# First stage of a two-block forward pass: input squares added on VectorE, block inverses of both directions joined, chunk matrices stored from GpSimd

## The chip, the core and the metric
One core of one Trainium2 chip runs the whole program in one launch. The metric is device time in microseconds, from start to end of the launch. Three runs of the kernel before took 2054.11, 2059.92 and 2060.92 us, so its median is 2059.92 us. Engines have short names in the rows: PE is TensorE (PEld its weight loads), DVE is VectorE, ACT is ScalarE, POOL is GpSimd, SP is SyncE, which here only issues DMAs.

## The reference, cut to what matters
Two transformer blocks over 1024 positions of width 1024, batch 1, in float32. The change lies in the first block, whose parts are

```python
h = rms_norm(x, norm_w)                       # sum of squares over the 1024 inputs
proj = h @ w_in                               # q, k, v, z, gates of the delta rule; q, k, v, z of attention
q, k = rotary(rms_norm(q)), rotary(rms_norm(k))   # windowed attention with sinks
m = where(strict, (k_beta @ k.T) * decay, 0)  # delta rule, chunk by chunk, forward and backward
t_inv = triangular_solve(eye + m, eye)        # unit triangular inverse of each chunk
u, w = t_inv @ (v * beta), t_inv @ (k_beta * exp(g))
a_intra = where(incl, (q @ k.T) * decay, 0)
```

where `decay` is exp of a difference of cumulated log gates. A scan over the chunks, an output norm, the output product and the second block follow; they are not touched.

## The kernel before, in words
The inputs are kept transposed: 8 row blocks of 128 input features (index k) by two halves of 512 positions (index h), 16 tiles of 128x512 in all. Each float32 operand of a projection is split into a rounded part and a rest (`hi`, `lo` for inputs, `wh`, `wl` for weights), and a product is the three matmuls of `mm3` (L219 to L221). The inputs are not scaled by the norm; its reciprocal `rcol` is applied when a product leaves PSUM.

The first stage runs in four parts, in the order of the code at the end of its block:

- `x_tile` loads the 16 tiles, splits them and sums their squares. Even k: ScalarE squares, VectorE adds (L746, L748). Odd k: GpSimd squares and adds (L744, L748). There are two sums for each half, and `norm_col` (L294) multiplies both with a column of ones; the result goes through `rsqrt` (L182 to L188), a chain of small VectorE steps, into `rcol`.
- Job `tg` (gates, attention keys and values), then `tq` twice (attention queries), each of 8 blocks of 128 positions. `kv_evac` and `q_evac` scale by `rcol`, square and sum by head (`sums`, L491, L492), and `rotated` (L496 to L512) applies norm weights and rotary tables, splits and transposes. `norm_row` spreads `rcol` to rows by copies `cb_a` (L302) and products `rb_a` (L303).
- Twelve jobs `fm` (delta rule q, k, v) with convolution and transposes, then `gate_terms`.
- Four jobs `ts`, `tz` (output gates). Between their matmuls stand the chunks: `m_chunk` makes for each of 8 chunks of 128 positions (two directions in one 128x512 tile, four heads) the decay `gam` from a product `pe`, the matrix `x_`, and two matrices `ta`; they are stored to `mdram` and `adram`. `base` reads the 16x16 diagonal blocks of four chunks back from `mdram` and inverts them by 15 rounds of a product `tmp` (L712) and a sum (L713), for each direction apart, starting from unit matrices that it loads (L706), and stores `cblk`.

The next stage needs the buffers of the first one, so its loads wait for the last `tz` matmul.

The order on each engine is not that of the code: a scheduler that runs a model of time while the program is built places the instructions. Every engine then works strictly in its own order, and an instruction that waits holds all behind it. DMAs issued from SP and ACT stand in those engines' orders too. Tags with a few buffers (`BUFS_A`) tie a writer to the last reader of the buffer.

Of the kernel before, what the change touches and what calls it, by code (L numbers as in the profile page):

```python
# [22 lines left out]
P = 128  # L23
# [10 lines left out]
BUFS_A = dict(wr=2, wh=6, wl=6, cv=4, acc=4, st=2, n1=4, n4=2, mb=1, tt=1, tmp=2)  # L34
# [78 lines left out]
def tile_two_blocks(ctx: ExitStack, tc: tile.TileContext, t, out, dbg=None, stop=None):  # L113
# [3 lines left out]
    dma, store = nc.sync.dma_start, nc.scalar.dma_start  # L117
# [308 lines left out]
    with ExitStack() as c1:  # L426
# [3 lines left out]
        def small(name, n, dt=F32):  # L430
# [15 lines left out]
        trir = pg.tile([P, 2, P], F32R, name="trir", tag="trir")  # L446
# [3 lines left out]
        GTr, LTr = trir[:, 0, :], trir[:, 1, :]  # L450
# [7 lines left out]
        with ExitStack() as ca:  # L458
# [15 lines left out]
            def tables():  # L474
                for nm, scale in (("k", 1.0), ("q", 0.125)):
                    wr = page("st", f"nw{nm}", [P, P])
                    dma(wr, t[f"swa_{nm}_norm_w"].partition_broadcast(P))
                    for i in range(2):
                        tb = page("cv", f"tab{nm}{i}", [P, NB, 64])
                        dma(tb, t["rope"][:, i])  # L480
                        if scale == 1.0:
                            G.tensor_tensor(tb, tb, rep(wr[:, i * 64 : (i + 1) * 64], NB), ALU.mult)
                        else:
                            if i == 0:
                                A.activation(wr, wr, AF.Copy, scale=scale)
                            G.tensor_tensor(tb, tb, rep(wr[:, i * 64 : (i + 1) * 64], NB), ALU.mult)
                        tabs[nm, i] = tb

            def sums(y, n, Hn, ss, name):
                sq = page("acc", f"sq{name}", [P, n, Hn, 64])  # L490
                G.tensor_tensor(sq, y, y, ALU.mult)  # L491
                V.tensor_reduce(ss, sq, AX.X, ALU.add)  # L492

            def rotated(y, rr, n, Hn, c, nm, name):
# [3 lines left out]
                for i in range(n):  # L498
                    G.tensor_tensor(t1[:, i], y[:, i], rep(tabs[nm, 0][:, c + i, :], Hn), ALU.mult)
                    for a in range(2):  # L500
                        V.tensor_tensor(
                            t2[:, i, :, 32 * a : 32 * a + 32], y[:, i, :, 32 - 32 * a : 64 - 32 * a],
                            rep(tabs[nm, 1][:, c + i, 32 * a : 32 * a + 32], Hn), ALU.mult,
                        )
                V.tensor_tensor(t1, t1, t2, ALU.add)
# [124 lines left out]
            def gate_terms():  # L630
# [13 lines left out]
                V.tensor_copy(ahi, av)  # L644
                V.tensor_tensor(alo, av, ahi.bitcast(F32), ALU.subtract)
# [15 lines left out]
            def m_chunk(gi, ci):  # L661
# [1333 lines left out]
```

## Time and profile before

| | us |
|---|---|
| median of three runs | 2059.92 |
| profiled execution | 2061.51 |
| its span, first to last instruction | 2059.5 |
| PE busy | 1943.0 (94%) |
| DVE busy | 1495.7 (73%) |
| ACT busy | 937.5 (46%) |
| POOL busy | 431.2 (21%) |

The profiled execution lies 1.6 us above the median, and its span 2.0 us below its own time. A share of busy time is a mean over stages with different limits, so the stage is to be read by stretches. The first stage is the first 398 us of the span.

### The profile page before, as it was taken

How to read it: one execution, taken by the hardware profiler on the slowest of the kernel's cores; microseconds unless marked ns; L12 is line 12 of the kernel's file. 1: busy time of each engine (PE TensorE's matmuls, PEld its weight loads, DVE VectorE, ACT ScalarE, POOL GpSimd, SP SyncE). 2: the span in 40 equal slices, each digit the busy share in tenths (PEclk: the TensorE clock that was granted, in tenths of full speed). 3: DMA queues.
4: the chain of work that ended last, by engine and by line, in shares of the span. 5: the costliest groups of instructions: out<-in, count | busy, mean ns of one | idle time of the engine just before them, and what ended most of it. 6: DMA issues, size and time to landing. Idle time of an engine off the chain costs nothing.

```text
span 2059.5 us, 31630 instructions
## 1 busy us (share of the span) xinstructions
PE 1943.0 (94%) x11446; PEld 1691.6 (82%) x11446; DVE 1495.7 (73%) x3087; ACT 937.5 (46%) x1954; POOL 431.2 (21%) x453
## 2 busy tenths in 40 slices
PE   6899988989988999799999799999999999999999
PEld 6888888889987789798999687686888888888887
DVE  7888888377797469563364888538977777776987
ACT  4446543134344253125553566525545445444443
POOL 5320073255252113011020762111000000000000
PEclk9999999999999999999999999999999999999999
DMA  5132334324535626743222223611222222267332
GB/s 167 41 122 75 89 113 129 98 52 144 150 105 191 233 82 181 238 140 101 61 85 59 79 65 89 226 49 59 84 92 82 72 92 82 72 214 277 98 97 83
DMA packets 177548, 235.13 MB, mean 114 GB/s; under 512 B 52944, under 2 KB 94064, under 8 KB 177392
## 3 DMA queue, kind: packets, MB, share of 16 engines
q1 hardware_dynamic: 148464, 205.84, 31.6%
q10 hardware_dynamic: 28928, 27.27, 4.0%
q8 instruction: 90, 1.47, 0.3%
q14 instruction: 66, 0.54, 0.1%
HBM read 174.86 MB, written 58.20 MB: 113 GB/s over the span
## 4 chain that ended last, share of the span: by engine, by line
PE 70%; DVE 15%; DMA 7%; issue 3%; ACT 3%; POOL 1%; SPq 0%; DVEq 0%; ACTq 0%; POOLq 0%
PE upx L219 4%; PE upx L220 4%; PE upx L221 4%; PE up L220 3%; PE up L221 3%; PE up L219 3%; DMA wa<-in_w_ada 2%; PE fm L220 2%; PE fm L219 2%; PE fm L221 2%; PE dnx L220 2%; PE dnx L219 2%; PE dnx L221 2%; PE apo L1241 1%; PE apt L1234 1%
## 5 line engine op out<-in xcount | busy, mean ns | idle before, releaser
L1587 ACT ACTIVATE uh<-wu 128x512 fp32r<-128x512 f32 x154 | 94.5, 628 | 143.0 <-DMA wu<-in_w_up 52.8
L1725 DVE SCALAR_TENSOR_TENSOR u<-c,fcw,u 128x1023 f32<-128x1023 f32 (+1 forms) x88 | 112.5, 1278 | 10.2 <-ACT u L1723 10.0
L1588 DVE TENSOR_TENSOR ul<-wu,uh 128x512 fp32r<-128x512 f32 x154 | 105.6, 698 | 4.7 <-ACT uh L1587 4.6
L210 DVE TENSOR_TENSOR wl<-wr,wh 128x512 fp32r<-128x512 f32 (+1 forms) x100 | 74.8, 755 | 43.9 <-ACT wh L209 43.3
L209 ACT ACTIVATE wh<-wr 128x512 fp32r<-128x512 f32 (+1 forms) x100 | 62.5, 630 | 94.6 <-PE fm L220 19.7
L403 DVE SCALAR_TENSOR_TENSOR aac<-wa,silc,aac 128x512 f32<-128x512 f32 x84 | 70.5, 839 | 37.1 <-DMA wa<-in_w_ada 32.6
L595 DVE SCALAR_TENSOR_TENSOR cacc<-raw,cw,cacc 128x512 f32<-128x512 f32 x96 | 70.5, 761 | 2.0 <-ACT cacc L593 0.6
L198 ACT ACTIVATE wdh<-w 128x512 fp32r<-128x512 f32 x55 | 34.8, 632 | 79.7 <-PE dnx L220 23.4
L220 PE MATMUL dnx<-bdl,wdh 128*128 128x512 f32 x176 | 68.6, 390 | 0.0
L221 PE MATMUL dnx<-bdh,wdl 128*128 128x512 f32 x176 | 68.5, 389 | 0.0
L1217 DVE CUSTOM_DVE_ANT_0 ass<-as,tb 128x512 f32<-128x512 f32 (+2 forms) x96 | 51.5, 552 | 23.4 <-PE as L1216 21.5
L1224 ACT ACTIVATE ass<-ass,amx 128x128 f32<-128x128 f32 (+3 forms) x64 | 49.3, 770 | 35.9 <-DVE amx L1223 33.8
L1723 ACT ACTIVATE u<-c,fcb,fcw 128x1024 f32<-128x1024 f32 x44 | 54.6, 1242 | 8.4 <-DVE c L1709 4.3
L199 DVE TENSOR_TENSOR bdl<-act,bdh 128x512 fp32r<-128x512 f32 x77 | 52.7, 684 | 1.8 <-ACT bdh L198 1.5
L220 PE MATMUL dny<-bdl,wdh 128*128 128x512 f32 x132 | 51.4, 389 | 0.0
L221 PE MATMUL dny<-bdh,wdl 128*128 128x512 f32 x132 | 51.4, 389 | 0.0
L836 ACT ACTIVATE ssb<-ssb,wnm 128x384 f32<-128x384 f32 (+1 forms) x64 | 36.8, 578 | 27.4 <-DVE wes L838 18.4
L219 PE MATMUL dnx<-bdh,wdh 128*128 128x512 f32 x176 | 48.9, 389 | 0.4 <-DVE dp L1898 0.4
L1234 PE MATMUL apt<-ident,ass 128*128 128x128 f32 x288 | 47.5, 280 | 1.7 <-ACT ass L1224 1.2
L198 ACT ACTIVATE bdh<-act 128x512 fp32r<-128x512 f32 x77 | 47.8, 621 | 2.1 <-issue 1.6
L863 PE MATMUL po<-sv,pTs 128*128 128x64 f32 x352 | 46.4, 271 | 1.5 <-DVE pTs L857 0.6
L199 DVE TENSOR_TENSOR wdl<-w,wdh 128x512 fp32r<-128x512 f32 x55 | 37.7, 686 | 13.4 <-ACT wdh L198 13.2
(2162 smaller groups left out, 7048.7 us busy)
## 6 DMA issues: line engine op xcount, KB each, us to landing
wu<-in_w_up SPq DMA_DIRECT2D x44, 512.0 KB, 3.3
wa<-in_w_ada SPq DMA_DIRECT2D x84, 256.0 KB, 3.5
adram<-u SPq DMA_DIRECT2D x22, 512.0 KB, 2.8
act<-adram SPq DMA_DIRECT2D x44, 256.0 KB, 5.6
wd<-in_w_down SPq DMA_DIRECT2D x20, 512.0 KB, 3.8
wr<-in_w_in_fm SPq DMA_DIRECT2D x24, 256.0 KB, 2.8
w<-in_w_down SPq DMA_DIRECT2D x22, 256.0 KB, 5.6
xt<-in_xT SPq DMA_DIRECT2D x16, 256.0 KB, 5.3
```

What stands on the lines that cost most here:

```text
L198: A.activation(hi, src, AF.Copy)
L199: marks["lo"] = V.tensor_tensor(lo, src, hi.bitcast(F32), ALU.subtract)
L210: V.tensor_tensor(lo, raw, hi.bitcast(F32), ALU.subtract)
L219: T.matmul(ps, ah, bh, start=first, stop=False, skip_group_check=more)
L220: T.matmul(ps, ah, bl, start=False, stop=False, skip_group_check=more)
L221: marks["mm3"] = T.matmul(ps, al, bh, start=False, stop=last, skip_group_check=more)
L403: V.scalar_tensor_tensor(aac, wa, silc[:, k : k + 1], aac, ALU.mult, ALU.add)
L595: V.scalar_tensor_tensor(acc, raw[h][:, j : j + H], cw[:, m, j : j + 1], acc, ALU.mult, ALU.add)
L1234: T.transpose(pt[:, u * P : (u + 1) * P], ss[i][:, g * P : (g + 1) * P], ident)
L1587: A.activation(hi, src, AF.Copy)
L1588: V.tensor_tensor(lo, src, hi.bitcast(F32), ALU.subtract)
L1725: V.scalar_tensor_tensor(u[:, sft:], cc[:, : S - sft], fcw[:, m, 2 - sft : 3 - sft], u[:, sft:], ALU.mult, ALU.add)
```

## The change
The squares are made by ScalarE for all k and added by VectorE into one sum for each half. The norm weight times rotary table is made by VectorE; the second table is loaded with its halves exchanged, in pieces of 32 numbers. `sums` squares on ScalarE. `rotated` makes both products over all blocks at once on VectorE and adds the halves crosswise. In `m_chunk` the gate is no longer split: `pe` is two float32 matmuls in place of four on rounded operands, one operand tile for each direction, both made by VectorE; `w1` is a ScalarE copy overwritten by a predicated VectorE copy under a byte mask; both `ta` are made by VectorE. The stores of `x_`, `ta` and `cblk` are issued from GpSimd. `base` holds the second direction reversed, so that one instruction serves both directions, and copies the unit matrices from a tile that is loaded once. GpSimd keeps some fills and casts and the diagonal fill and transposing copy at the end of `base`.

```diff
-    dma, store = nc.sync.dma_start, nc.scalar.dma_start
+    dma, store, pdma = nc.sync.dma_start, nc.scalar.dma_start, nc.gpsimd.dma_start
...
             def tables():
...
+                    tb = tabs[nm, 0] = page("cv", f"tab{nm}0", [P, NB, 64])
+                    dma(tb, t["rope"][:, 0])
+                    V.tensor_tensor(tb, tb, rep(wr[:, 0:64], NB), ALU.mult)
+                    tb = tabs[nm, 1] = page("cv", f"tab{nm}1", [P, NB, 64])
+                    for a in (0, 32):
+                        half = tb[:, :, a : a + 32]
+                        dma(half, t["rope"][:, 1, :, 32 - a : 64 - a])
+                        V.tensor_tensor(half, half, rep(wr[:, 96 - a : 128 - a], NB), ALU.mult)
...
-                G.tensor_tensor(sq, y, y, ALU.mult)
+                A.activation(sq, y, AF.Square)
...
-                for i in range(n):
-                    G.tensor_tensor(t1[:, i], y[:, i], rep(tabs[nm, 0][:, c + i, :], Hn), ALU.mult)
-                    for a in range(2):
-                        V.tensor_tensor(
...
-                V.tensor_tensor(t1, t1, t2, ALU.add)
+                tab = lambda i: tabs[nm, i][:, c : c + n, :].unsqueeze(2).to_broadcast([P, n, Hn, 64])
+                V.tensor_tensor(t1, y, tab(0), ALU.mult)
+                V.tensor_tensor(t2, y, tab(1), ALU.mult)
+                for a in (0, 32):
+                    half = t1[:, :, :, a : a + 32]
+                    V.tensor_tensor(half, half, t2[:, :, :, 32 - a : 64 - a], ALU.add)
...
-                    for part in (ahi.bitcast(F32), alo):
-                        r_ = page("n1", f"rr{c}{len(rr)}", G4, F32R)
-                        (G if d == 0 else V).tensor_tensor(r_, rep(mat, 4), bc(part[:, c, 4 * d : 4 * d + 4], P), ALU.mult)
-                        rr.append(r_)
-                w1, w2 = page("acc", f"w1{c}", G4), page("acc", f"w2{c}", G4)
-                G.tensor_tensor(w1, rep(LT, 4), bc(wgt[:, c, 0:4], P), ALU.mult)
-                G.tensor_tensor(w2, rep(GT, 4), bc(wgt[:, c, 4:8], P), ALU.mult)
-                V.tensor_tensor(w1, w1, w2, ALU.add)
+                    r_ = page("n1", f"rr{c}{d}", G4)
+                    V.tensor_tensor(r_, rep(mat, 4), bc(av[:, c, 4 * d : 4 * d + 4], P), ALU.mult)
+                    rr.append(r_)
+                w1 = page("acc", f"w1{c}", G4)
+                A.activation(w1, bc(wgt[:, c, 0:4], P), AF.Copy)
+                V.copy_predicated(w1, rep(gtm, 4), bc(wgt[:, c, 4:8], P))
...
-                for i, mat in enumerate((GTr, GTr, LTr, LTr)):
-                    T.matmul(pe, mat, rr[i], start=i == 0, stop=i == 3)
+                for i, mat in enumerate((GT, LT)):
+                    T.matmul(pe, mat, rr[i], start=i == 0, stop=i == 1)
...
-                dma(m_view(gi, ci), x_)
+                pdma(m_view(gi, ci), x_)
...
-                    (G if d == 0 else V).tensor_tensor(tt, gam, rep(mat, 4), ALU.mult)
-                    dma(adram[c, d], tt.rearrange("p h d -> p (h d)"))
+                    V.tensor_tensor(tt, gam, rep(mat, 4), ALU.mult)
+                    pdma(adram[c, d], tt.rearrange("p h d -> p (h d)"))
...
+                V.tensor_scalar(mb[:, 0].rearrange("p j i -> p (j i)"), raw, -1.0, None, ALU.mult)
+                V.tensor_scalar(mb[:, 1].rearrange("p j i -> p (j i)"), raw[:, ::-1], -1.0, None, ALU.mult)
                 tt = page("tt", f"tt{gi}", [P, 2, 16, 16])
-                for d in range(2):
-                    dma(tt[:, d].rearrange("p r c -> p (r c)"), t["eye16"].partition_broadcast(P))
+                A.activation(tt.rearrange("p d r c -> p d (r c)"), rep(eye, 2), AF.Copy)
                 for q in range(1, 16):
-                    for d in range(2):
...
+                    tmp = page("tmp", f"tmp{gi}{q}", [P, 2, 15, 15])[:, :, 0:q, 0:q]
+                    V.tensor_tensor(tmp, tt[:, :, 0:q, 0:q].rearrange("p d j c -> p d c j"), mb[:, :, 0:q, q].unsqueeze(2).to_broadcast([P, 2, q, q]), ALU.mult)
+                    V.tensor_reduce(tt[:, :, q, 0:q], tmp, AX.X, ALU.add)
...
                 for u in range(2):
-                    dma(cblk[gi, u].rearrange("(q r c) -> q r c", q=P, r=16), tt[:, u])
+                    pdma(cblk[gi, u].rearrange("(q r c) -> q r c", q=P, r=16), tt[:, u])
...
-                if odd:
-                    G.tensor_tensor(sq, xt, xt, ALU.mult)
+                if k == 0:
+                    xsum[h] = page("acc", f"xacc{h}")
+                    A.activation(xsum[h], xt, AF.Square)
                 else:
-                    A.activation(sq, xt, AF.Square)
-                if k >= 2:
-                    (G if odd else V).tensor_tensor(xacc[h][odd], xacc[h][odd], xt, ALU.add)
+                    A.activation(xt, xt, AF.Square)
+                    V.tensor_tensor(xsum[h], xsum[h], xt, ALU.add)
```

The code's edits also move instructions on the engines. The first place is VectorE's order around the norm chain of the first half of positions (`ru_n`, `rcol`), where `xacc` is the sum of squares, `x17l` the rest of the last tile and `tabq` the rotary table of the queries. Before:

```order
L210 TENSOR_TENSOR wl_288<-wr_286,wh_287 128x512
L188 SCALAR_TENSOR_TENSOR rcol<-ru_n_340,rcol 128x4
L748 TENSOR_TENSOR xacc_222<-xacc_222,xt_264 128x512
L186 TENSOR_TENSOR ru_n_340<-rcol 128x4
L737 SCALAR_TENSOR_TENSOR x17l<-xt_272,norm_w,x17h 128x512
L187 SCALAR_TENSOR_TENSOR ru_n_340<-ru_n_340,rv_n_338 128x4
L188 SCALAR_TENSOR_TENSOR rcol<-ru_n_340,rcol 128x4
L186 TENSOR_TENSOR ru_n_340<-rcol 128x4
L187 SCALAR_TENSOR_TENSOR ru_n_340<-ru_n_340,rv_n_338 128x4
L188 SCALAR_TENSOR_TENSOR rcol<-ru_n_340,rcol 128x4
L524 TENSOR_SCALAR gates<-tg_304,rcol 128x16
```

And VectorE's order there in the changed kernel:

```order
L739 TENSOR_TENSOR xacc_221<-xacc_221,xt_255 128x512
L188 SCALAR_TENSOR_TENSOR rcol<-ru_n_335,rcol 128x4
L739 TENSOR_TENSOR xacc_221<-xacc_221,xt_263 128x512
L186 TENSOR_TENSOR ru_n_335<-rcol 128x4
L480 TENSOR_TENSOR tabq_589<-tabq_589,nwq 128x512
L739 TENSOR_TENSOR xacc_221<-xacc_221,xt_271 128x512
L187 SCALAR_TENSOR_TENSOR ru_n_335<-ru_n_335,rv_n_333 128x4
L485 TENSOR_TENSOR tabq_592<-tabq_592,nwq 128x8x32
L188 SCALAR_TENSOR_TENSOR rcol<-ru_n_335,rcol 128x4
L186 TENSOR_TENSOR ru_n_335<-rcol 128x4
L485 TENSOR_TENSOR tabq_592<-tabq_592,nwq 128x8x32
L187 SCALAR_TENSOR_TENSOR ru_n_335<-ru_n_335,rv_n_333 128x4
```

More sums of squares and the products of the query table, which wait for the table's loads, now stand between the steps of the norm chain; the chain of the second half follows directly behind it.

The second place is VectorE's order where the copies `cb_a` for the row form of the norm stand among the query heads (`qy` scaled by its norm, `t1q`, `t2q` the rotary products). Before:

```order
L496 TENSOR_TENSOR qy_824<-qy_824,rrq_1023 128x512
L496 TENSOR_TENSOR qy_880<-qy_880,rrq_1023 128x512
L496 TENSOR_TENSOR qy_936<-qy_936,rrq_1023 128x512
L496 TENSOR_TENSOR qy_992<-qy_992,rrq_1023 128x512
L541 CAST khh_109<-ptk_725 64x128
L501 TENSOR_TENSOR t2q_1041<-qy_824,tabq_599 128x4x32 x4
L302 COPY cb_a_753<-rcol 128x128
L501 TENSOR_TENSOR t2q_1073<-qy_880,tabq_599 128x4x32
L541 CAST khh_108<-ptk_737 64x128
L501 TENSOR_TENSOR t2q_1073<-qy_880,tabq_599 128x4x32
L302 COPY cb_a_756<-rcol 128x128
```

And in the changed kernel:

```order
L302 COPY cb_a_733<-rcol 128x128
L187 SCALAR_TENSOR_TENSOR ru_dn<-ru_dn,rv_dn 128x32
L188 SCALAR_TENSOR_TENSOR rrq_1000<-ru_dn,rrq_1000 128x32
L494 TENSOR_TENSOR qy_801<-qy_801,rrq_1000 128x512
L494 TENSOR_TENSOR qy_857<-qy_857,rrq_1000 128x512
L494 TENSOR_TENSOR qy_913<-qy_913,rrq_1000 128x512
L494 TENSOR_TENSOR qy_969<-qy_969,rrq_1000 128x512
L497 TENSOR_TENSOR t1q_1017<-qy_801,tabq_589 128x512
L498 TENSOR_TENSOR t2q_1018<-qy_801,tabq_592 128x512
L497 TENSOR_TENSOR t1q_1046<-qy_857,tabq_589 128x512
L498 TENSOR_TENSOR t2q_1047<-qy_857,tabq_592 128x512
L302 COPY cb_a_738<-rcol 128x128
```

The third and fourth copies (`cb_a_730`, `cb_a_733`) now stand ahead of the four `qy`, and the next pair stands behind eight full instructions.

The third place is SP's order at the end of the chunks, where `mb` (now `mr`) is the read of the diagonal blocks. Before:

```order
L695 DMA adram<-ta_3327 128x512
L695 DMA adram<-ta_3324 128x512
L701 DMA mb_3330<-mdram 128x16x16
L720 DMA cblk<-tt_3081 128x256 x2
L706 DMA tt_3333<-in_eye 128x256 x2
L208 DMA wr_3927<-in_w_in_z 128x512
```

And in the changed kernel:

```order
L208 DMA wr_3491<-in_w_in_z 128x512
L208 DMA wr_3497<-in_w_in_z 128x512
L693 DMA mr_3174<-mdram 128x16x16
L208 DMA wr_3727<-in_w_in_z 128x512
```

No store and no load of unit matrices stands in SP's order any more.

## Rows read from the trace of the kernel before
**Rows 1.** The page: busy tenths in 40 slices of the span.
```profile
PE   6899988989988999799999799999999999999999
POOL 5320073255252113011020762111000000000000
```
**Rows 2.** Windows: busy us of each engine in five stretches, granted PE clock, DMA.
```profile
8.40:42.40 34.00, 25.55 (x163) 24.10 (x163) 33.51 (x45) 18.11 (x32) 23.78 (x17) 0.93 0.64 202
42.40:50.80 8.40, 8.40 (x48) 8.40 (x49) 2.01 (x3) 2.75 (x8) 3.38 (x3) 0.69 0.01 2
50.80:112.00 61.20, 54.39 (x438) 53.66 (x437) 47.01 (x138) 28.37 (x83) 21.64 (x28) 0.94 0.19 60
112.00:263.30 151.30, 151.30 (x731) 124.12 (x730) 132.09 (x270) 80.17 (x232) 13.91 (x33) 1.00 0.29 89
263.30:397.80 134.50, 119.61 (x925) 116.43 (x923) 94.27 (x200) 48.24 (x69) 59.44 (x44) 0.95 0.39 119
```
**Rows 3.** Timeline of PE: start us, us, instruction, idle before and what ended it.
```profile
60.19 0.39 PE L219 MATMUL tq<-wh,x00h 128*128 128x256 f32 x1 [1.14 <-ACT ky L529]
93.54 0.80 PE L303 MATMUL rb_a<-ident,cb_a 128*128 128x128 f32 x2 [5.10 <-DVE cb_a L302]
```
**Rows 4.** Timeline of DVE, 8 to 93 us.
```profile
28.85 1.78 DVE L737 SCALAR_TENSOR_TENSOR x15l<-xt,norm_w,x15h 128x512 fp32r<-128x512 f32 x1
33.69 1.25 DVE L183 TENSOR_SCALAR ri_n<-rv_n 128x4 int32<-128x4 int32 x1
36.21 1.18 DVE L186 TENSOR_TENSOR ru_n<-rcol 128x4 f32<-128x4 f32 x1
41.37 0.66 DVE L524 TENSOR_SCALAR gates<-tg,rcol 128x16 f32<-128x16 f32 x4
56.44 0.16 DVE L186 TENSOR_TENSOR ru_n<-rcol 128x4 f32<-128x4 f32 x1
87.94 3.55 DVE L496 TENSOR_TENSOR qy<-qy,rrq 128x512 f32<-128x512 f32 x4
```
**Rows 5.** Groups of DVE by shape, 0 to 62 us: busy us, mean ns.
```profile
L748 DVE TENSOR_TENSOR xacc<-xacc,xt 128x512 f32<-128x512 f32 x6 | 7.5, 1251 | 0.1
```
**Rows 6.** Groups of DVE by shape, 262 to 347 us.
```profile
L673 DVE TENSOR_TENSOR w<-w,w 128x512 f32<-128x512 f32 x8 | 10.3, 1290 | 1.9 <-POOL w L672 1.9
L668 DVE TENSOR_TENSOR rr<-tri,alo 128x512 fp32r<-128x512 f32 x7 | 10.1, 1436 | 0.0
L684 DVE TENSOR_TENSOR x<-pgr,gam 128x512 f32<-128x512 f32 x8 | 5.5, 682 | 0.7 <-ACT gam L679 0.7
```
**Rows 7.** Groups of POOL by shape, 260 to 350 us.
```profile
L671 POOL TENSOR_TENSOR w<-tri,wgt 128x512 f32<-128x512 f32 x8 | 12.0, 1495 | 5.8 <-DVE x L685 5.8
```
**Rows 8.** Waits of PE, 263 to 398 us: us in total, times, longest.
```profile
PE tz L220 <- DVE wl L210: 4.7, 1, 4.7
PE pe L677 <- DVE tmp L712: 4.1, 2, 2.5
PE ts L219 <- ACT s L573: 2.1, 1, 2.1
PE pqk L690 <- ACT gam L679: 2.0, 2, 1.1
```
**Rows 9.** Chain that ended last, 345 to 355 us: start us, us, what.
```profile
346.48 2.62 DMA cblk<-tt
349.57 4.43 DMA tt<-in_eye
```
**Rows 10.** Groups of PE by shape, 100 to 400 us; the third from the second block.
```profile
L677 PE MATMUL pe<-rr,trir 128*128 128x512 f32 x32 | 9.8, 418 | 6.0 <-DVE tmp L712 4.1 <-DVE x L684 1.9
L682 PE MATMUL pgr<-qk 128*128 128x128 f32 x64 | 8.7, 276 | 0.0
L1359 PE MATMUL pla<-glrT,wg 16*128 16x512 f32 x8 | 5.7, 851 | 4.2 <-DVE gl L1367 4.2
```
**Rows 11.** DMA issues, 300 to 400 us: KB each, median us to landing.
```profile
mdram<-x SPq DMA_DIRECT2D x5, 256.0 KB, 2.3
```

More of the change, by code (lines that the diff above doesn't have):

```diff
@@ L434, in tile_two_blocks @@
         ssk, ssq, rk, rkinv, rk2, rq = (small(n, 4) for n in ("ssk", "ssq", "rk", "rkinv", "rk2", "rq"))
-        beta, av, ahi, alo, wgt, neg, edec, egl, eg = (
-            small(n, 8, F32R if n == "ahi" else F32) for n in ("beta", "av", "ahi", "alo", "wgt", "neg", "edec", "egl", "eg")
-        )
+        beta, av, wgt, neg, edec, egl, eg = (small(n, 8) for n in ("beta", "av", "wgt", "neg", "edec", "egl", "eg"))
         rcol = pg.tile([P, NB], F32, name="rcol", tag="rcol")
@@ L449, in tile_two_blocks @@
         GT, LT, LE, GE = (tri[:, i, :] for i in range(4))
-        GTr, LTr = trir[:, 0, :], trir[:, 1, :]
         groups = ([0, 7, 1, 6], [2, 5, 3, 4])
@@ L477, in tables @@
                     dma(wr, t[f"swa_{nm}_norm_w"].partition_broadcast(P))
[L478 to L487, printed above, removed]
+                    if scale != 1.0:
+                        A.activation(wr, wr, AF.Copy, scale=scale)
+                    tb = tabs[nm, 0] = page("cv", f"tab{nm}0", [P, NB, 64])
[6 more added lines that the diff above has]
+                        V.tensor_tensor(half, half, rep(wr[:, 96 - a : 128 - a], NB), ALU.mult)
             def sums(y, n, Hn, ss, name):
                 sq = page("acc", f"sq{name}", [P, n, Hn, 64])
-                G.tensor_tensor(sq, y, y, ALU.mult)
+                A.activation(sq, y, AF.Square)
                 V.tensor_reduce(ss, sq, AX.X, ALU.add)
@@ L518, in kv_evac @@
                 if c == 0:
-                    norm_col(pbt, xacc[0], rcol[:, 0:4], "a0")
+                    norm_col(pbt, [xsum[0]], rcol[:, 0:4], "a0")
                     ys["ss"] = sm.tile([P, NB, 2], F32, name="ssk2", tag="ss2")
                 if c == 4:
-                    norm_col(pbt, xacc[1], rcol[:, 4:8], "a1")
+                    norm_col(pbt, [xsum[1]], rcol[:, 4:8], "a1")
                 r1 = rcol[:, c : c + 1]
@@ L716, in base @@
                 G.memset(tt[:, 1].rearrange("p r c -> p (r c)")[:, ::17], 0.0)
-                V.tensor_tensor(tt[:, 0], tt[:, 0], tt[:, 1], ALU.add)
+                V.tensor_tensor(
+                    tt[:, 0].rearrange("p r c -> p (r c)"), tt[:, 0].rearrange("p r c -> p (r c)"),
+                    tt[:, 1].rearrange("p r c -> p (r c)")[:, ::-1], ALU.add,
+                )
                 G.tensor_copy(tt[:, 1], tt[:, 0].rearrange("p r c -> p c r"))
                 for u in range(2):
-                    dma(cblk[gi, u].rearrange("(q r c) -> q r c", q=P, r=16), tt[:, u])
+                    pdma(cblk[gi, u].rearrange("(q r c) -> q r c", q=P, r=16), tt[:, u])
                 yield
@@ L728, in tile_two_blocks @@
             nw = load(pg, "norm_w", [P, NK], t["norm_w"])
-            xacc = [[None, None] for _ in range(2)]
+            xsum = {}
+            eye = page("eye", "eye", [P, 256])
             def x_tile(h, k):
@@ L738, in x_tile @@
                 xs[k][h] = (hi, lo)
-                odd = k % 2
-                if k < 2:
-                    xacc[h][odd] = page("acc", f"xacc{h}{k}")
-                sq = xacc[h][odd] if k < 2 else xt
-                if odd:
-                    G.tensor_tensor(sq, xt, xt, ALU.mult)
-                else:
-                    A.activation(sq, xt, AF.Square)
-                if k >= 2:
-                    (G if odd else V).tensor_tensor(xacc[h][odd], xacc[h][odd], xt, ALU.add)
+                if k == 0:
+                    xsum[h] = page("acc", f"xacc{h}")
+                    A.activation(xsum[h], xt, AF.Square)
+                else:
+                    A.activation(xt, xt, AF.Square)
+                    V.tensor_tensor(xsum[h], xsum[h], xt, ALU.add)
             def consts():
@@ L757, in consts @@
                 dma(tri, t["tri"])
+                dma(eye, t["eye16"].partition_broadcast(P))
                 dma(onw, t["dn_out_norm_w"].partition_broadcast(P))
-                G.tensor_copy(trir, tri[:, 0:2, :])
+                G.tensor_copy(gtm, GT)
                 for g in range(2):
```

20 lines of the change are left out of this document (5 added, 15 removed).

## The prediction
> **What bounds the kernel now.** I read the page's slices first [rows 1]: PE is near full almost everywhere, and POOL works above all in the first eight slices, which hold the first stage. Then the windows [rows 2], cut where the stage's parts begin and end. From 112 to 263.3 us PE is busy 151.30 of 151.30 us at full clock; nothing that the change touches can shorten this stretch, since its matmuls stay. PE's idle time lies elsewhere: 34.00 - 25.55 = 8.4 us up to 42.4, 61.20 - 54.39 = 6.8 us up to 112, and 134.50 - 119.61 = 14.9 us in the last stretch. To this comes the clock: after an idle stretch PE runs for a few us at the lower of its two levels (1.2 for 2.4 GHz); the granted share is 0.69 between 42.4 and 50.8, 0.94 and 0.95 in two longer ones. So the stage is bound by PE where PE is fed, and by VectorE where it is not: in the first window VectorE is busy 33.51 of 34.00 us.
>
> Why VectorE is slow there is seen in its own rows. A norm step of 128x4 numbers takes 1.25 and 1.18 us next to GpSimd's work, and 0.16 us at 56.44, where POOL stands still [rows 4]. Six additions of 128x512 have a mean of 1.25 us [rows 5]. In the chunks `w<-w,w` takes 1.29 and `rr` 1.44 us, while `x<-pgr,gam`, of the same size with one operand in PSUM, takes 0.68 us in the mean of eight and is never held up [rows 6]. GpSimd's instruction beside them takes 1.5 us [rows 7]. I take 0.68 us as the undisturbed length of a 128x512 instruction; such instructions overlap by some 0.08 us, so 0.6 us each in a row.
>
> **The change part by part.** All against the profiled execution's 2061.5 us.
>
> *Start, to the gates at 41.37 us [rows 4].* What goes: the six additions lose 6 x (1.25 - 0.68) = 3.4 us [rows 5]; four norm steps of the kind shown lose 1 us each, 4 us; five splits of inputs and two of weights of the kind of `x15l` (1.78 us [rows 4]) lose some 0.9 us each, 6 us. Sum 13.4 us. What comes: eight more additions, 8 x 0.6 = 4.8 us, and four table products' worth of 512 numbers, 2.4 us. Net -6 us on VectorE. The table products wait for loads, and the norm chain is queued behind them in VectorE's order; behind the chain stand the gates and the evacuations that give PE its PSUM back. The loads need buffers that the additions free late, so the last one lands some 3 us after its addition, against 1 to 2 us of work between them: I take back 1.5 us (bounds 0, and the whole 6 us if every table load is waited for). ScalarE gets eight more squares and a copy; at 18.11 us of 34 [rows 2] it takes 5 us more without being the bound. Net 4.5 us.
>
> *Second half's norm.* Its chain now follows directly, so PE's wait of 1.14 us at 60.19 [rows 3] goes: 1 us.
>
> *Row form of the norm.* PE waits 5.10 us for `cb_a` at 93.54 [rows 3], behind four `qy` that take 3.55 us [rows 4] and a run of `t2q`. In the new order a pair of copies stands ahead of them and the next pair eight instructions later (4.8 us), while PE has a block's 24 products between the pairs, 3 us. A wait of 1.5 us stays, 3.5 us go, and with them part of the stretch at the lower level that follows, which I put at 1 us: 4.5 us.
>
> *Fifteen rounds of `base`, other `rotated`, single norm sum.* `base` does the same numbers in half as many instructions, each now dependent on the one before; I put it at nothing, covered by other VectorE work between its steps; uncovered, 30 steps at 0.1 us would cost 3 us. `rotated` adds about 0.4 us for each call on VectorE, under PE's full stretch. Halving the norm's matmuls is worth under 1 us and lies in idle time: nothing.
>
> *Chunks.* On VectorE each chunk had 7 instructions and has 8 (one predicated copy for one addition, one `ta` more), 8 x 0.6 = 4.8 us more in all. The excess in [rows 6] goes: 8 x 0.6 + 7 x 0.75 = 10 us for two groups alone; with the other `rr`, `ta` and the small steps of `base` that I counted on the timeline it is 22 us. No row has a predicated copy; by the nearest rows it lies between 0.3 us, half of the undisturbed 0.68, and 1.4 us, the slowest two-operand group [rows 6], and I take 0.6. So VectorE gains 17 us here (11 to 20). PE pays: `pe` was four products, 9.8 / 8 = 1.2 us for a chunk. Float32 costs more: `pgr`, float32 with 512 columns in all, is 8.7 / 8 = 1.1 us, so two such are 2.2 us, +1.0 each and at most +8 in eight chunks; the other float32 row of 512 columns, partly at the lower level, is 5.7 / 4 = 1.4 us [rows 10], +13. I take 7 us, as part of these busy times is overlap.
>
> What PE can gain in this stretch is its 14.9 us of idle time and some 6 us for the clock (0.95 means that a tenth of 134.5 us ran at half speed). The `pe` waits, 4.1 us, should go; so should 4.7 us for `wl` [rows 8]. That one is VectorE held in its order by the load of unit matrices, 2.62 + 4.43 us after the blocks' store began [rows 9]; these loads no longer exist. What is late next is the read `mr` of the last chunks: it, the copy of the unit matrices and seven rounds stand ahead of the same `wl`, and by the old durations they fit into the 15 us that PE has work for, with about 2 us to spare. The waits for ScalarE's `s` and `gam`, 2.1 and 2.0 us, stay [rows 8]. Of 21 us I count 15 as regained, less 7 for `pe`: 8 us.
>
> *Stores from GpSimd.* 24 of `x_` and `ta`, 4 of `cblk`. SP's landing took 2.3 us [rows 11]. GpSimd has nothing else to do; no row shows a DMA issued there. Bounds: no more than SP's, so nothing, and 1.5 us each, the length of its arithmetic [rows 7], which makes 36 us spread over 60 us of chunks, still hidden. I take nothing, with the rival below.
>
> The Trainium skill weighs against this part: its page "SBUF — State Buffer" (section "SBUF: two separate sides") says that a DMA issued from GpSimd has its descriptors written there, and that these writes are locked out while VectorE runs certain copies in a two-port mode. The same page ("Who interferes with whom") counts `copy` and `tensor_scalar` among those, and not `tensor_tensor`. By it only the few sign changes of `base` would hold a store up, so the sum would be the same; the trace of before has no store from GpSimd and cannot say.
>
> Sum: 4.5 + 1 + 4.5 + 8 = 18 us, some 0.5 us more for stalls in between that I did not price: 2061.5 - 18.5 = 2043 for an execution like the profiled one, which lies 1.6 us above its median. So 2041 us. The order behind the first stage is nearly the old one, and I take no difference from it.
>
> **Rivals.**
> *The start gains nothing.* The table loads, in small pieces of 32 numbers, are waited for one after another, and the norm chain behind them is as late as before. For it: the order shown. Against it: the loads' queues are idle after 34 us. The chunks' 8 us and the row form's 4.5 us stay at best; with half of the latter, 2051 us.
> *The chunks gain nothing.* Float32 `pe` at the upper price, 13 us, eats what is regained, or VectorE with 64 us of work in a stretch of some 60 us of PE work stays the bound. For it: both engines come out almost equal. Then only the 10 us before remain: 2050 us.
> *Slower: stores from GpSimd become the bound.* If each takes over 2.5 us of GpSimd, 24 of them fill the 60 us of the chunks; `x_` and `ta` wait for their buffers, VectorE for them, PE for VectorE. Each further us costs 24 us. The rest of the gain, 18 us, is used up at about 3.3 us each; at 4 us it would be 2061 + 18 = 2077 us. For it: the page's rule, if it held for all of VectorE's work. Against it: SP's 2.3 us is mostly transfer, not issue.
> *It does not do what it says*: the diagonal fill and the transposing copy stay on GpSimd, but only twice; the rows show no other.
>
> **How the numbers follow.** My case has 0.62, 2041 us, own range 2032 to 2050. Start without gain 0.16, 2051. Chunks without gain 0.13, 2050. Slower 0.06, 2077. Nothing moves 0.03. More than my case is bounded by PE: all idle time but the first 8 us and all clock losses, less `pe`, would be some 29 us, 2031. The range 2030 to 2056 leaves out the slower rival and part of the tails. A change of over 0.3% (6.2 us), about what a measurement of this kernel can tell, means below 2053.7: 0.61 of my case, 0.11 and 0.11 of the two weaker ones, 0.83. Within 0.3%: 0.10. Slower: 0.07.
>
> **What would show it.** In the windows, the stretch up to the first `fm` matmul should be 10 us shorter, that of `ts`, `tz` and the chunks 8 us, the middle unchanged. No 128x4 step of VectorE above 0.3 us; `rr` and `ta` near 0.68 us. Gates near 37 us. The wait of `rb_a` under 2 us, none of `tz` for `wl`. `pe` above 1.9 us for a chunk. I am wrong if `tabq` is waited for by more than 3 us, if a store from GpSimd needs over 2.5 us before it starts, or if PE still idles over 8 us in the last stretch.

## The result and the profile after

The changed kernel takes 2026.14 us in the median of four runs, against 2059.53 us: ratio 0.984, interval 0.981 to 0.988. Two more comparisons gave 0.985 (0.982 to 0.987) and 0.984 (0.982 to 0.986). It is faster by 31 to 35 us, where 18.5 were forecast. Its profiled execution takes 2027.40 us (span 2025.6), 34.1 us less than that of before.

The page's slices of the changed kernel, against [rows 1]: POOL's first five slices are below a tenth, and PE's first seven at least as full as they were.

```profile
PE   7999999899989998899999899999999999999999
POOL 0000021563351123021022742110000000000000
```

The windows of the changed kernel, cut at the same events as [rows 2]; the columns are busy us of PE, PEld, DVE, ACT and POOL, PE's granted clock, the DMA share and GB/s:

```profile
8.40:37.90 29.50, 23.37 (x160) 22.03 (x160) 27.03 (x63) 22.23 (x41) 0.64 (x1) 0.96 0.74 225
37.90:50.80 12.90, 12.82 (x87) 12.82 (x88) 5.74 (x21) 8.95 (x24) 0.00 (x0) 0.82 0.15 43
50.80:102.80 52.00, 49.20 (x407) 49.01 (x406) 40.64 (x109) 29.05 (x81) 1.33 (x4) 0.97 0.21 71
102.80:253.20 150.40, 150.40 (x724) 123.50 (x724) 129.81 (x267) 81.43 (x231) 2.21 (x22) 1.00 0.29 88
253.20:373.70 120.50, 118.58 (x929) 111.02 (x928) 72.75 (x146) 50.99 (x75) 20.84 (x35) 1.00 0.46 137
373.70:474.90 101.20, 91.56 (x738) 87.78 (x737) 80.21 (x165) 36.30 (x93) 65.86 (x58) 0.95 0.27 76
```

The last three stretches of before, cut at the same events, for the comparison (the first of them ends with the first `ts` matmul, the second with the last `tz`, which starts at 399.66, 2 us behind the end of the last stretch of [rows 2]):

```profile
114.20:265.30 151.10, 151.10 (x727) 123.70 (x726) 131.85 (x269) 79.62 (x228) 15.57 (x35) 1.00 0.29 88
265.30:399.90 134.60, 119.71 (x927) 116.58 (x925) 92.33 (x198) 47.07 (x67) 57.78 (x43) 0.95 0.40 118
399.90:505.00 105.10, 93.91 (x739) 90.00 (x739) 81.43 (x167) 36.30 (x93) 66.39 (x58) 0.94 0.30 81
```

Read by these cuts, the time went so (all from PE's timelines of the two profiled executions, between starts of matmuls; `pc` is a product of the next stage):

| stretch | before | after | measured | forecast |
|---|---|---|---|---|
| start to first `fm` | 114.2 | 102.9 | -11.3 | -10 |
| first `fm` to first `ts` | 151.2 | 150.3 | -0.8 | 0 |
| first `ts` to last `tz` | 134.3 | 120.2 | -14.1 | -8 |
| last `tz` to last `pc` of the next stage | 104.3 | 100.4 | -3.9 | 0 |
| all behind it | 1555.6 | 1551.8 | -3.8 | 0 |

The last row is scatter: three traces of the changed kernel have 1551.8, 1558.2 and 1550.6 us there. In the first row 1.3 to 2.3 us of before are scatter too: three variants that leave the start as it was begin their first `fm` at 111.85 to 112.85. Between the means of the four traces with the old start and the ten with the new one lie 9.7 us. The third and fourth rows are larger than any scatter seen in them, and the forecast missed both.

VectorE's rows of the changed kernel at the start, against [rows 4]; no small step is above 0.2 us, and `gates` come at 36.97:

```profile
26.18 0.16 DVE L183 TENSOR_SCALAR ri_n<-rv_n 128x4 int32<-128x4 int32 x1
33.81 0.69 DVE L480 TENSOR_TENSOR tabq<-tabq,nwq 128x512 f32<-128x512 f32 x1 [0.73 <-DMA tabq<-in_rope]
36.97 0.66 DVE L520 TENSOR_SCALAR gates<-tg,rcol 128x16 f32<-128x16 f32 x4
```

VectorE's groups by shape, 0 to 62 us, against [rows 5], and 250 to 374 us, against [rows 6]:

```profile
L739 DVE TENSOR_TENSOR xacc<-xacc,xt 128x512 f32<-128x512 f32 x14 | 9.7, 691 | 0.1
...
L686 DVE TENSOR_TENSOR ta<-gam,tri 128x512 f32<-128x512 f32 x16 | 10.3, 684 | 0.1
L661 DVE TENSOR_TENSOR rr<-tri,av 128x512 f32<-128x512 f32 x12 | 8.1, 686 | 0.3 <-PE pe L669 0.3
L665 DVE COPY_PREDICATED w<-gtm,wgt 128x512 f32<-128x512 uint8 x8 | 5.9, 736 | 5.8 <-ACT w L664 5.8
L676 DVE TENSOR_TENSOR x<-pgr,gam 128x512 f32<-128x512 f32 x8 | 5.4, 677 | 0.0
```

PE's waits from 253 to 374 us, all that are left (us in total, times, longest), against [rows 8]:

```profile
PE pqk L682 <- ACT gam L671: 1.2, 2, 0.8
PE pf L600 <- ACT cacc L593: 0.4, 1, 0.4
PE pe L669 <- DVE x L676: 0.3, 1, 0.3
```

`pe` as a group of PE, 250 to 374 us, against [rows 10] (the trace has two records for each of the 16 float32 products):

```profile
L669 PE MATMUL pe<-rr,tri 128*128 128x512 f32 x32 | 15.3, 595 | 0.3 <-DVE x L676 0.3
```

The stores as groups of GpSimd in the same stretch (busy us, mean ns):

```profile
L687 POOL DMA_DIRECT2D adram<-ta x16 | 8.7, 542 | 8.9 <-DVE ta L686 8.3 <-issue 0.2
L678 POOL DMA_DIRECT2D mdram<-x x8 | 6.2, 780 | 59.4 <-DVE x L677 41.5 <-DVE tt L704 18.0
```

and as DMA issues (KB each, median us to landing), against [rows 11]:

```profile
adram<-ta POOLq DMA_DIRECT2D x16, 256.0 KB, 2.6
mdram<-x POOLq DMA_DIRECT2D x8, 256.0 KB, 2.8
cblk<-tt POOLq DMA_DIRECT2D x4, 128.0 KB, 3.4
```

### The profile page after: what moved, and what is told of

Same layout as the page of the kernel before. It is cut to its first block, busy times and chain, and to the rows that moved or that the text cites. A ratio compares the mean times of both kernels' runs of the same rounds, so it can differ in the third digit from the quotient of the medians.

```text
span 2025.6 us, 31441 instructions
## 1 busy us (share of the span) xinstructions
PE 1938.5 (96%) x11430; PEld 1683.3 (83%) x11430; DVE 1457.2 (72%) x3031; ACT 952.8 (47%) x1982; POOL 334.0 (16%) x389
## 4 chain that ended last, share of the span: by engine, by line
PE 74%; DVE 12%; DMA 7%; ACT 3%; issue 3%; SPq 1%; POOL 0%; ACTq 0%; DVEq 0%; POOLq 0%
PE upx L220 4%; PE upx L221 4%; PE upx L219 4%; PE up L220 3%; PE up L221 3%; PE up L219 3%; DMA wa<-in_w_ada 2%; PE fm L219 2%; PE fm L221 2%; PE fm L220 2%; PE dnx L220 2%; PE dnx L219 2%; PE dnx L221 2%; PE po L855 1%; PE apo L1233 1%
## 5 line engine op out<-in xcount | busy, mean ns | idle before, releaser
L828 ACT ACTIVATE ssb<-ssb,wnm 128x384 f32<-128x384 f32 (+1 forms) x64 | 36.8, 578 | 29.4 <-DVE wes L830 18.5
L855 PEld LDWEIGHTS po<-sv,pTs 128*128 128x128 f32 x352 | 46.3, 200 | 2.9 <-DVE pTs L849 1.4
```

The costliest lines, as they stand in the source:

```text
L855: T.matmul(po[:, h, :], pts[i][:, h, :], sv[:, kb, g * 64 : (g + 1) * 64], start=i == 0, stop=kb == kb1 - 1)
```

## The experiments

Those that begin with `b_` edit the kernel before, those with `a_` the changed one. In the three traces of the changed kernel the first 474 us repeat within 2 us, while the rest scatters over 8 us; so single parts are judged by PE's timeline in the first stage, and the time is given beside it.

**The changed kernel again.**

> The changed kernel once more, for its time against the kernel before and for a second trace. Theory: 2026 us (1.6% less than before), with 30 us of the difference ahead of the first matmul of the next stage's second part and nothing real behind it; the 3.8 us that the first pair of traces shows behind 505 us (of before) are then scatter between executions and come out between -4 and +4 here. Rival: the change moves the later stages too (other addresses of tiles, other order), and the same 3 to 4 us stand at the same places again.

> The changed kernel once more, beside its variant with the split gate on the same chip. 2024 to 2029 us; first fm matmul within 1 us of 102.6, first ts to last tz 120.2, both as in its two traces so far.

Measured: 2026.07 and 2025.15 us; first `fm` at 102.38 and 101.59, first `ts` to last `tz` 120.23 and 119.90, last `pc` at 473.2 and 472.0 (473.8 in the first trace). Behind it 1558.2 and 1550.6 us, against 1555.6 in the trace of before: 2.6 more and 5.0 less. The gain lies in the first 505 us; the later 3.8 us did not come again as such, as the theory said.

**One part at a time.** The start alone (the edits of `x_tile`, `tables`, `sums`, `rotated`):

```diff
-                G.tensor_tensor(sq, y, y, ALU.mult)
+                A.activation(sq, y, AF.Square)
...
+                V.tensor_tensor(t1, y, tab(0), ALU.mult)
+                V.tensor_tensor(t2, y, tab(1), ALU.mult)
```

> The kernel before with the part of the change ahead of the fm jobs alone: squares on ScalarE with one VectorE sum, tables multiplied on VectorE, sums and rotated as changed; chunks and base as before. Theory (the parts add up): first fm matmul at 103 us as in the changed kernel, 11 us earlier than before; the stretch from the first ts to the last tz matmul stays at 134 us and PE still waits 4 to 5 us for wl and 4 us at pe; in all 10 to 12 us less than before. Rival (a later wait takes the gain): the time falls by under 5 us, with the 11 us lost again in a longer stretch of ts and tz.

Measured: 2050.18 us against 2058.80, 8.6 less (ratio 0.996, 0.994 to 0.997), a little under the 10 to 12 expected. First `fm` at 104.17, 10.0 earlier than the profiled before and 7.7 to 8.7 earlier than in `b_addr`, `b_base` and `b_chunks`, which keep the old start; first `ts` to last `tz` 134.05. Nothing is taken back later. The two longest waits of PE, 250 to 392 us:

```profile
PE pe L676 <- DVE tmp L711: 6.4, 2, 3.3
PE tz L220 <- DVE wl L210: 5.0, 1, 5.0
```

The chunks' arithmetic alone, with stores on SP and `base` as before:

```diff
-                        (G if d == 0 else V).tensor_tensor(r_, rep(mat, 4), bc(part[:, c, 4 * d : 4 * d + 4], P), ALU.mult)
+                    V.tensor_tensor(r_, rep(mat, 4), bc(av[:, c, 4 * d : 4 * d + 4], P), ALU.mult)
...
-                    (G if d == 0 else V).tensor_tensor(tt, gam, rep(mat, 4), ALU.mult)
+                    V.tensor_tensor(tt, gam, rep(mat, 4), ALU.mult)
```

> The kernel before with the arithmetic of the chunks alone as changed: rr, the copy and predicated copy, both ta on VectorE, pe in two float32 products; stores stay on SP, base and the start as before. Theory (GpSimd's arithmetic beside VectorE held VectorE up): VectorE's 128x512 instructions take 0.68 us, the waits at pe (4.1 us) go, the wait of tz for wl (4.7 us) stays in some measure since base still loads its unit matrices: the stretch from first ts to last tz gets 6 to 9 us shorter than 134.3. Rival (the chunks gain only together with base): under 3 us shorter, since the small instructions of base keep VectorE as late as before.

Measured: 2048.14 us against 2058.80, 10.7 less (0.995, 0.993 to 0.996). The stretch from `ts` to `tz` is 126.00, 8.3 shorter. All of PE's waits in it:

```profile
PE tz L220 <- DVE wl L210: 5.6, 1, 5.6
PE pf L601 <- ACT cacc L594: 0.5, 1, 0.5
PE pqk L683 <- ACT gam L672: 0.3, 1, 0.3
```

The waits at `pe` are gone, and so are those for ScalarE's `s` and `gam` but for 0.3 us, which the forecast let stand; the wait behind the load of unit matrices stays.

`base` alone:

```diff
-                for d in range(2):
-                    dma(tt[:, d].rearrange("p r c -> p (r c)"), t["eye16"].partition_broadcast(P))
+                A.activation(tt.rearrange("p d r c -> p d (r c)"), rep(eye, 2), AF.Copy)
```

> The kernel before with base alone as changed: both directions in one instruction, unit matrices copied by ScalarE from a tile that is loaded once (into a part of rrow that is no longer read by then); chunks' arithmetic on GpSimd as before, stores on SP. The weights move by 2 KB too, so cmp is loaded early. Theory (the wait of 4.7 us for wl is the load of the unit matrices): this wait goes, the waits at pe stay within 1 us of 4.1, the stretch from first ts to last tz is 4 to 6 us shorter than 134.3. Rival (VectorE, held up by GpSimd, is the true cause of that wait): the stretch is under 2 us shorter.

Measured: 2048.66 us against 2058.80, 10.1 less (0.996, 0.994 to 0.997). The stretch is 129.68, 4.6 shorter. The wait of 4.7 us for `wl` is gone (1.1 us for `wh` is left). At `pe` PE waits 7.1 us:

```profile
PE pe L677 <- DVE x L684: 3.8, 3, 3.0
PE pe L677 <- DVE tmp L714: 3.3, 1, 3.3
```

That is no growth. The 4.1 us of my expectation are only the waits behind `tmp`; before has one more, behind `x`, which [rows 8] does not show (its 1.9 us stand in the first line of [rows 10]):

```profile
PE pe L677 <- DVE x L684: 1.9, 1, 1.9
```

So before waits 6.0 us at `pe`, and `b_addr` below, whose order is that of before, 7.1:

```profile
PE pe L677 <- DVE tmp L714: 6.5, 2, 3.4
PE pe L677 <- DVE x L684: 0.6, 2, 0.3
```

`base` also joins the two directions here, so the load of the unit matrices is not tested apart from that.

The parts add up: 8.3 + 4.6 = 12.9 of the 14.1 us of this stretch, and 10.0 of 11.3 at the start, both from the same late trace of before. The times of the three parts add up to 29.4 us of 31 to 35; in `b_base` half of the 10.1 us lies outside the stretch: its weights move too, and from the last `tz` to the last `pc` it takes 98.2 us against 104.3 before.

**Is it GpSimd's arithmetic as such, or waiting for its results?** First the stores back on SP, as a base for the two that follow:

```diff
-    dma, store, pdma = nc.sync.dma_start, nc.scalar.dma_start, nc.gpsimd.dma_start
+    dma, store, pdma = nc.sync.dma_start, nc.scalar.dma_start, nc.sync.dma_start
```

> The changed kernel with all stores of chunk matrices and block inverses issued from SP as before. Theory (the issuer is worth nothing, as predicted): within 2 us of the changed kernel; PE keeps under 3 us of idle time between the first ts and the last tz matmul. Rival (stores in SP's order hold up the loads of the weights and of mr, as the wait of 4.7 us for wl before): PE waits for wl again, 4 to 8 us more than the changed kernel.

Measured: 2029.40 us, beside 2026.07 of the changed kernel (ratios 0.987, 0.984 to 0.989, and 0.985, 0.982 to 0.987): 3.3 us more, where within 2 us was expected, and not told apart. First `ts` to last `tz` 119.93, last `pc` at 474.06, both as with GpSimd; PE waits 0.90 us for `wl`. The issuer is worth nothing in the first stage, though the stores land later from GpSimd: here from SP 2.2, 2.4 and 1.8 us after issue, from GpSimd 2.6, 2.8 and 3.4 (`ta`, `x_`, `cblk`).

Then products on GpSimd that nobody waits for:

```diff
+            nz = [rrow[:, 0:H], rrow[:, H:S]]
...
+                G.tensor_tensor(nz[0].rearrange("p (h d) -> p h d", h=4), rep(LT, 4), bc(wgt[:, c, 0:4], P), ALU.mult)
+                G.tensor_tensor(nz[1].rearrange("p (h d) -> p h d", h=4), rep(GT, 4), bc(wgt[:, c, 4:8], P), ALU.mult)
```

> The variant with stores from SP (a_sp), and in each chunk five products of 128x512 more on GpSimd, into a tile that nobody reads: as many as the kernel before had there. The order on the other engines is that of a_sp, and nothing waits for these products. Theory (GpSimd's arithmetic as such holds VectorE up): VectorE's instructions with both operands in SBUF (rr, x<-x,w, ta) rise from 0.69 to 1.1 to 1.4 us in the mean, those with one operand in PSUM stay at 0.68; PE waits again, the stretch from first ts to last tz matmul grows from 119.9 to 126 to 132 us and its clock falls under 1.00; time 6 to 12 us more. Rival (what cost time before was waiting for GpSimd's late results): the means stay, the stretch is less than 1 us longer.

Measured: 2046.07 us (ratio to before 0.993, 0.992 to 0.995), 17 to 21 us more than without. The window from first `ts` to last `tz`, of this variant:

```profile
254.40:391.70 137.30, 124.09 (x929) 113.56 (x928) 96.52 (x150) 52.75 (x79) 54.67 (x43) 0.96 0.41 124
```

and its groups of VectorE by shape, 250 to 380 us:

```profile
L692 DVE TENSOR_TENSOR ta<-gam,tri 128x512 f32<-128x512 f32 x16 | 15.4, 1004 | 0.1
L662 DVE TENSOR_TENSOR rr<-tri,av 128x512 f32<-128x512 f32 x12 | 14.9, 1264 | 0.0
L668 DVE COPY_PREDICATED w<-gtm,wgt 128x512 f32<-128x512 uint8 x8 | 10.9, 1359 | 1.4 <-ACT w L667 1.4
...
L681 DVE TENSOR_TENSOR x<-pgr,gam 128x512 f32<-128x512 f32 x8 | 5.4, 679 | 0.0
```

Nothing depends on these products, and VectorE's order is the same; yet its work in this stretch grows from 73 to 97 us, the clock falls to 0.96, and the stretch is 136.9 us long, more than expected and more than before the change (the mean of `ta`, 1.00 us, is a little under the range expected). The instruction with an operand in PSUM is untouched at 0.68 us. PE waits 8.4 us at `pe` for `x` and 1.5 for `gam` again; `a_sp` has neither wait. The rival is out.

Last, fills in place of the products:

```diff
-                G.tensor_tensor(nz[0].rearrange("p (h d) -> p h d", h=4), rep(LT, 4), bc(wgt[:, c, 0:4], P), ALU.mult)
+                G.memset(nz[0], 0.0)
+                G.memset(nz[0], 0.0)
```

> As a_noise, but with ten fills of 128x512 on GpSimd in each chunk in place of the five products: GpSimd writes as much and reads no operand. Theory (it is GpSimd's reading of operands that VectorE waits for): VectorE's means stay within 0.05 us of 0.69, the stretch from first ts to last tz stays within 1 us of 119.9. Rival (any access of GpSimd to SBUF will do): the means rise over 0.9 us and the stretch grows by 4 us or more.

Measured: 2029.19 us. The window of this variant:

```profile
253.90:373.90 120.00, 118.65 (x928) 111.01 (x928) 73.28 (x146) 50.89 (x75) 36.21 (x77) 1.00 0.47 138
```

and two of the same groups of VectorE:

```profile
L662 DVE TENSOR_TENSOR rr<-tri,av 128x512 f32<-128x512 f32 x12 | 8.2, 688 | 0.4 <-PE pe L678 0.3
L670 DVE COPY_PREDICATED w<-gtm,wgt 128x512 f32<-128x512 uint8 x8 | 5.9, 740 | 6.0 <-ACT w L669 6.0
```

GpSimd is busy for 36 us here and holds nobody up. So what VectorE pays for is GpSimd's reading of operands in SBUF, by VectorE's own instructions with both operands there. The Trainium skill, "SBUF — State Buffer" (section "Who interferes with whom"), states this rule for two-input instructions of VectorE against a GpSimd instruction that reads, and not one that only writes; both runs agree, with 1.26 against 0.69 us for `rr`. One row does not fit "both operands": `ri_n`, a step of 128x4 with a single tensor operand, took 1.25 us beside GpSimd before [rows 4] and 0.16 after; no run here tests it alone.

**Where does the seam between the stages come from?** By the layout of the built program the tile `cmp`, the first load of the next stage, lies at the same address in both kernels, but the weight tiles of the first stage moved by some 2 KB (`mr`, the larger `mb` behind them). Before, `cmp` lies on weights of the last `tz` job; after, on those of the job ahead of it. No trace shows addresses, so this is tested by its effect: two variants move the weights alone; the order on each engine is unchanged.

```diff
+                if gi == 0:
+                    page("pad", "pad", [P, 512])
```

> The kernel before with 2 KB per partition of unused memory at the end of the first stage's pool; the order on every engine is the same. It only moves the weight tiles by 2 KB, so that the tile cmp of the next stage lies on weights that are read some 10 us before the stage's end and no longer on those of the last matmuls. Theory (the gain of 3.8 us at the seam between the stages is a matter of addresses): the load cmp<-cblk starts some 8 us ahead of the last tz matmul, PE's wait of 2.44 us for r and the slow first products go, time 3 to 4 us under that of before. Rival (the seam gains because the blocks' inverses are stored earlier, or because SP's queue is empty): no difference, within 1 us.

```diff
             eye = page("eye", "eye", [P, 256])
+            page("mb", "mb_", [P, 2, 16, 16])
```

> The changed kernel with the slot of mb laid out ahead of the weights and not behind them; the order on every engine is the same. The weight tiles stand within 32 bytes of where they stood before the change, so that cmp lies on weights of the last tz matmuls again. Theory (addresses): the load waits for the last tz matmul again, PE waits 2 to 3 us for r, 3 to 4 us more than the changed kernel (2029 to 2030). Rival (earlier store of the inverses, or SP's queue): no difference, within 1 us.

The timeline of the load's issue on SP and of the first product `px` on PE, of the kernel before:

```profile
397.84 1.54 SPq L891 DMA_DIRECT2D cmp<-cblk  x2
...
408.61 1.35 PE L927 MATMUL px<-p,l 128*128 128x128 f32 x8 [2.36 <-DVE l L901]
```

The same of `b_addr`:

```profile
388.27 2.87 SPq L893 DMA_DIRECT2D cmp<-cblk  x2
...
402.61 1.13 PE L929 MATMUL px<-p,l 128*128 128x128 f32 x8 [2.06 <-DVE l L903]
```

Of the changed kernel:

```profile
363.95 2.59 SPq L883 DMA_DIRECT2D cmp<-cblk  x2
...
378.60 1.13 PE L919 MATMUL px<-p,l 128*128 128x128 f32 x8 [2.92 <-DVE l L893]
```

Of `a_addr`:

```profile
370.68 1.60 SPq L884 DMA_DIRECT2D cmp<-cblk  x2
...
381.37 3.61 PE L920 MATMUL px<-p,l 128*128 128x128 f32 x16 [2.46 <-DVE l L894]
```

The last `tz` matmul starts at 399.66, 397.40, 373.39 and 372.49. So the load is issued 1.8, 9.1, 9.4 and 1.8 us ahead of it, and `px` comes 8.95, 5.21, 5.21 and 8.88 us behind it: 3.7 us at the seam, set by the address alone. By the last `pc` some is given back, and 2.8 us are left between before and `b_addr`, 1.2 between the other two. The other traces fall in line: where `px` comes 5.2 us behind the last `tz` (ten traces), the last `pc` comes after 98.2 to 101.4 us; where it comes 8.8 to 9.0 us behind (before, `b_start`, `b_chunks`, `a_addr`), after 101.6 to 104.5. The times are 2057.55 us against 2057.22 for `b_addr` (0.998 to 1.001) and 2030.02 against 2026.07 for `a_addr` (intervals overlap); 3 us cannot be read from them, and for `b_addr` they show no gain. Shown is the seam in the trace, not its worth in the end.

`a_addr` shows one thing more that was not expected. Its stretch from first `ts` to last `tz` takes 117.92 us, 2.3 less than that of the changed kernel, with 0.4 us of idle time on PE:

```profile
254.57:372.50 117.93, 117.48 (x927) 110.54 (x925) 71.51 (x144) 51.08 (x75) 20.71 (x34) 1.00 0.43 132
```

So tile addresses alone moved this stretch by some 2 us in this trace; why, stays open.

**The price of the float32 `pe`.** The gate split again, all four operand tiles made by VectorE:

```diff
-                for i, mat in enumerate((GT, LT)):
-                    T.matmul(pe, mat, rr[i], start=i == 0, stop=i == 1)
+                for i, mat in enumerate((GTr, GTr, LTr, LTr)):
+                    T.matmul(pe, mat, rr[i], start=i == 0, stop=i == 3)
```

> The changed kernel with the gate split again: four products on rounded operands for pe, their four operand tiles all made by VectorE (two instructions more for each chunk); the kept unit matrix and the mask lie in parts of rrow that are no longer read. Theory (the float32 pe costs PE 5.5 us in a stretch that PE bounds, and VectorE has slack): pe takes 1.2 us of PE for a chunk in place of 1.9, the stretch from first ts to last tz is 3 to 5.5 us shorter than in the changed kernel (120.2). Rival (16 instructions of 0.69 us more, 11 us, make VectorE late): PE waits at pe again and the stretch is as long or up to 4 us longer.

> The variant with the split gate (a_f32r) once more. Its trace was 5.4 us ahead of the changed kernel at 470 us, its time from another comparison was not. Theory (the gain is real, and the later stages scatter by more): 3 to 6 us less than the changed kernel beside it. Rival (the later stages take the gain back): the same time within 2 us, with the lead lost again at one place that the two traces show.

Measured: first `ts` to last `tz` 116.56 and 117.66, 3.6 and 2.5 us shorter than 120.2 (3 to 5.5 were expected), and last `pc` at 468.0 and 470.4. `pe` in the first of them, as a group of PE:

```profile
L678 PE MATMUL pe<-rr,trir 128*128 128x512 f32 x31 | 8.7, 400 | 0.0
```

VectorE has room for the 16 instructions more (83.2 us of 116.6). PE's busy time falls from 118.6 to 112.7 us, but its idle time grows from 1.9 to 3.8, of which 2.0 are a wait for `gam`. The times are 2028.97 us against 2058.80 of before (0.986, 0.984 to 0.987) and 2024.62 beside 2025.15 of the changed kernel (0.983, 0.982 to 0.984, beside 0.984, 0.982 to 0.986). They do not tell the two apart, and the 3 to 6 us less that the second text expects did not come. The price in PE's busy time is shown, 15.3 against 8.7 us for `pe`, with both stretches at full clock. That the shorter stretch comes of it is not: this variant moves tiles too, and `a_addr`, with the two float32 products, is as short within 0.3 to 1.4 us. No variant here is shown to beat the changed kernel.

## Why the prediction was wrong

The direction and the mechanism were right; two terms of the sum were mis-sized: the time regained in the chunks' stretch, and the seam behind it, put at nothing. Of the spans' difference of 33.9 us, 15.4 were not forecast: 6.1 in the chunks' stretch, 3.9 at the seam, 1.3 at the start, 0.8 in the `fm` jobs, 3.8 of scatter behind, less the 0.5 for stalls that I had added without a place. Up to the last `tz` the two traces differ by 26.2 us, still under the 29 us that I took as the most; what lies behind it, 3.9 us at the seam and the scatter, carried the time below the range.

- *Start to the gates, 4.5 us*: 41.37 to 36.97, 4.4 us. The table loads are waited for by 0.73 and 0.41 us, within the 1.5 us taken back. With the second half's norm and the row form the forecast was 10 us; 9.7 us lie between the means of the traces. That sum is in part luck. The wait of 5.1 us at `rb_a` is gone, but 2.8 us for `qy` at 83.06 came in its place (ScalarE's `qy` waits for the first `t2q`, which stands behind the four `qy` on VectorE, 2.49 us): 2.3 us regained of 3.5. The clock made up for it: by the granted shares of the windows from 8.4 us to the first `fm` it cost some 8.7 us before and 5.1 after, an estimate that gives 3.6 us gained where I had 1.
- *"Of 21 us I count 15 as regained"* is the step that failed. Regained were 14.1 + 5.5 = 19.6. Idle time fell from 14.9 to 1.9 us, and with it all of the clock's loss: PE's busy time fell by 1.1 us in spite of 5.5 us more of `pe`, and the granted clock is 1.00. Of the 6 us that I did not count, 4.1 are the waits for ScalarE's `s` and `gam`, which I had let stand as another engine's matter; the other 1.9 have no place in the sum, and as much is PE's wait at `pe` for `x`, which [rows 8] leaves out. All of them fell with VectorE's delay in `b_chunks`: `pe` no longer waits, and of the others 0.3 us for `gam` is left. For `x` the cause is shown, since `a_noise` brings it back. For `gam` it is likely (1.5 us in `a_noise` and none in `a_sp`, but 1.2 in the changed kernel itself). For `s` it is not shown: `a_noise` has no such wait, and in variants that leave the chunks alone it is 0.6 (`b_start`) to 1.5 us (`b_base`).
- *`pe`, 7 us more*: 9.8 to 15.3, 5.5 us; the 9.8 stood in a stretch with a granted clock of 0.95, and against the 8.7 us of `a_f32r`, at 1.00, it is 6.6. *VectorE, 17 us less*: 92.3 to 72.8, 19.6. *Predicated copy, 0.6 us*: 0.74.
- *Wait for `wl`, 4.7 us, held by the load of unit matrices*: it stays in `b_chunks` and goes in `b_base`, which halves the instructions of `base` as well.
- *Stores from GpSimd, nothing*: right. 0.54 and 0.78 us of GpSimd each, landing 2.6 and 2.8 us after issue against 2.2 and 2.4 in `a_sp`, whose stretch is as long. They are far from the 2.5 us at which the slower rival began.
- *"The order behind the first stage is nearly the old one, and I take no difference from it"* failed too: the order is the old one, but here a load's start hangs on which tile last lay at its address. Nor do the next stage's loads wait for the last `tz` matmul, as the description of the kernel before says: `cmp` was issued 1.8 us ahead of its start before and 9.4 after. That could have been read before, from the 1.8 us between `cmp<-cblk` and the end of the stage, and from sizes that the change adds to a pool.
- The rivals that the start or the chunks gain nothing fell with `b_start` and `b_chunks`. What I set against the first, that the loads' queues are idle after 34 us, is not so: the DMA share is 0.35 and 0.44 in the two pieces of 2 us from 38 to 42. The range's lower end, 2030, rested on 29 us to be had from PE's idle time and clock ahead of 398 us, and left out the seam behind it.

## What to carry to other kernels

Where GpSimd reads SBUF beside VectorE, price all that VectorE's lateness drags along: waits named after other engines and the clock can go with it, as here, so count the whole idle time of such a stretch and name what would keep each part of it. When an edit changes the sizes of tiles, look which tile of the next stage lies on which of this one. And price a part by a trace cut at the same events, since the time of this kernel scatters by more than most parts are worth.

## What was not expected of the hardware

A predicated copy of 128x512 under a byte mask is held up like a two-operand instruction (0.74 to 1.36 us beside GpSimd's products). The delay is larger than I took it for: 39 products, 57 us of GpSimd's time, cost VectorE 23 us and the stretch 17 us. The price of float32 on PE was about as forecast: two matmuls of 512 columns cost 1.9 us per chunk, four on rounded operands 1.1 at full clock (`a_f32r`). And tile addresses alone moved a stretch in which the order was the same by 2.3 us (`a_addr`).
